# Loading the scan's row broadcasts through GpSimd's queue instead of SyncE's

## The chip, the cores and the metric

The kernel runs on one core of a Trainium2 chip. The metric is the device time of one execution in microseconds (us), as the median of several runs; lower is better. The engines are PE (TensorE, matmuls), DVE (VectorE), ACT (ScalarE), POOL (GpSimd) and SP (SyncE, which here issues DMAs only). Each engine works through its own queue in order; semaphores order the engines among themselves.

## The reference, cut to what matters

One layer of a bidirectional encoder on a sequence of 512 tokens with 1024 features, all in float32. The part that matters is branch A, a state-space scan in both directions with 32 heads in 4 groups, in chunks of 128 tokens:

```
a_cum  = cumsum(dt * a_head)                 # within a chunk, for each head and direction
decay  = exp(where(lower, a_cum[l] - a_cum[s], -inf))
y_diag = einsum(c.b, decay, x * dt)          # inside a chunk
y_off  = einsum(c, h_in, exp(a_cum))         # from the state that enters the chunk
y      = y_fwd + y_bwd + d_skip * x
```

Around it stand one wide input projection, a depthwise convolution, windowed attention, a gated merge, cross-attention into a memory of 256 tokens, and a feed-forward block.

## The kernel before, in words

**Weights.** Every weight block is 128 x 1024 float32 (512 KB). `load` (line 117) fetches it by `nc.sync.dma_start` into a buffer `raw` (two of them), casts it to a high part `whi` (ACT, line 130) and takes the rest as `wlo` (DVE or POOL, line 131); three buffers each. `mac` (line 135) multiplies with three matmuls per 128 x 128 block (lines 140 to 142). A load is written two weights ahead of the step that uses it.

**Projections of the scan.** `conv` (line 401) reads a projection from PSUM with one ACT instruction and four of DVE (`cvu`, line 409), then a tanh. PSUM has three banks for such projections, so PE waits when DVE has not emptied one.

**The rows.** `dt_step` writes the cumulated decays of all 64 (head, direction) pairs, 64 x 512, to DRAM as `adr`, and their exponentials as `edr`. In the scan these are read back, broadcast over partitions:
- `rows(h)` (line 510) loads for one head both directions of `adr` into `rt`, 128 x 2 x 512 (512 KB), with three buffers (`RB = 3`). `head` (line 526) asks for it, masks each direction on POOL (`affine_select`, line 532) and exponentiates on ACT (eight instructions, line 539). `both` (line 542) adds the directions on POOL into `mt` (line 545), which frees the `rt` buffer. `times` multiplies on DVE (line 550), and `inner` (line 554) feeds PE (line 560).
- `earows(i)` (line 517) loads `edr` for two heads into the two halves of `ear`, two DMAs of 64 x 2 x 512 (256 KB each), two buffers. `gather` (line 576) multiplies and adds them to the output `vv` on DVE and POOL (lines 584 and 585), which frees the buffer.

POOL also makes the weighted inputs `xw` of the state (line 490), sums of `bs` (line 643) and some squares, and it issues the twelve stores of the cross-attention's keys and values, `kdr` and `vdr` (lines 259 and 279).

**Order.** For each of the four groups, the scan's steps are woven by hand (`order`, `weave`) with the projections of the next group, the gates, and the output projection of the group before. The instructions are then laid into each engine's queue by a planner that simulates the kernel's times: of the instructions that are ready for an engine at that time, the earliest written goes first. So an instruction's place in a queue depends on the times that the planner expects. All loads before the change, weights and rows, stand in SP's one queue.

Of the kernel before, what the change touches and what calls it, by code (L numbers as in the profile page):

```python
# [15 lines left out]
P = 128  # L16
D = 1024
S = 512
# [55 lines left out]
def bidir_hybrid_layer(ctx: ExitStack, tc: tile.TileContext, io, dbg=None):  # L74
    nc = tc.nc
# [16 lines left out]
    adr = dram.tile([64, S], F32, tag="adr", name="adr")  # L92
    edr = dram.tile([64, S], F32, tag="edr", name="edr")
# [390 lines left out]
    def group_scan(g):  # L484
# [25 lines left out]
        def rows(h):  # L510
            rt = st["sp"].tile([P, 2, S], F32, tag="rt", name="rt", bufs=RB)
            e0 = 8 * g + h
            nc.sync.dma_start(rt, adr.rearrange("(d e) s -> e d s", d=2)[e0:e0 + 1].broadcast_to([P, 2, S]))
            st["rt", g, h] = rt


        def earows(i):
            def f():
                st["ear", i] = ear = st["sp"].tile([P, 2, S], F32, tag="ear", name="ear", bufs=2)
                for k in range(2):  # L520
                    e0 = 8 * g + 2 * i + k
                    nc.sync.dma_start(ear[64 * k:64 * k + 64], edr.rearrange("(d e) s -> e d s", d=2)[e0:e0 + 1]
                                      .broadcast_to([64, 2, S]))
            return f

        def head(h):
            def f():
                for n in (range(RB) if h == 0 else [h + RB - 1] if h + RB - 1 < HPG else []):
                    rows(n)
                rt = st["rt", g, h]  # L530
                for d in range(2):
                    nc.gpsimd.affine_select(  # L532
                        out=rt[:, d].rearrange("p (c l) -> p c l", c=NCH),
                        in_=rt[:, d].rearrange("p (c l) -> p c l", c=NCH), pattern=[[0, NCH], [1 - 2 * d, P]],
                        base=0, channel_multiplier=2 * d - 1, compare_op=ALU.is_ge, fill=neg)
                for d in range(2):
                    for c in range(NCH):
                        r, e0 = rt[:, d, c * P:(c + 1) * P], 32 * d + 8 * g + h
                        nc.scalar.activation(r, r, AF.Exp, bias=st["nb"][:, c, e0:e0 + 1])  # L539
            return f  # L540
# [690 lines left out]
```

## Time and profile before

| | |
|---|---|
| median of 3 runs | 1307.06 us (1306.88 to 1308.92) |
| the profiled execution | 1304.91 us |
| its span, first to last instruction | 1303.1 us |
| mean granted TensorE clock | 0.991 |
| busy: PE | 1251.0 us (96% of the span) |
| busy: DVE, ACT, POOL | 772.1 (59%), 564.3 (43%), 313.2 (24%) us |
| bytes moved by DMA | 143.48 MB, mean 110 GB/s |

The scan lies between about 90 and 510 us. Times in the rows are us from the start of the span, unless marked ns. A busy time counts computing instructions; issuing a DMA is not counted as busy. "<-" behind a wait names what ended it. The granted clock is given as a share of TensorE's full 2.4 GHz.

### The profile page before, as it was taken

The numbers are of one execution on the slowest core, as the hardware profiler recorded it, in microseconds if no ns is written. First come the engines' busy times: TensorE is split into PE (matmuls) and PEld (weight loads), VectorE is DVE, ScalarE is ACT, GpSimd is POOL, SyncE is SP. The second block draws the span as 40 slices with busy tenths as digits, with TensorE's granted clock in tenths as the row PEclk, the third lists the DMA queues.
The fourth block names the chain that finished last, engine by engine and source line by source line (L and its number), as shares of the span: only waits on it lengthen the run. The fifth ranks groups of instructions, "written<-read, shape, count | busy, mean of one in ns | idle before, by whom it ended". The sixth has DMA issues, their size and how long they took to land.

```text
span 1303.1 us, 16244 instructions
## 1 busy us (share of the span) xinstructions
PE 1251.0 (96%) x6076; PEld 1011.3 (78%) x6076; DVE 772.1 (59%) x1226; ACT 564.3 (43%) x1062; POOL 313.2 (24%) x259
## 2 busy tenths in 40 slices
PE   6988999999999999999999999999999999999996
PEld 5776678778778688877667888888888888888886
DVE  5874797677778865688874345675444444432323
ACT  6546655365465232358883234444332222222220
POOL 2344552442671732210000002001111111110001
PEclk9998999999999999999999999999999999999998
DMA  6447364445354232330104333422223222333331
GB/s 228 160 119 196 130 188 148 120 153 141 106 153 137 81 114 80 120 97 33 50 27 139 99 103 107 126 65 65 97 92 98 94 98 95 98 98 94 94 97 65
DMA packets 49614, 143.48 MB, mean 110 GB/s; under 512 B 5120, under 2 KB 8576, under 8 KB 49536
## 3 DMA queue, kind: packets, MB, share of 16 engines
q1 hardware_dynamic: 47248, 138.32, 34.7%
q10 hardware_dynamic: 1584, 2.03, 0.5%
q0 software_dynamic: 704, 2.10, 0.4%
q8 instruction: 48, 0.79, 0.3%
q14 instruction: 30, 0.25, 0.1%
HBM read 137.97 MB, written 4.46 MB: 109 GB/s over the span
## 4 chain that ended last, share of the span: by engine, by line
PE 59%; issue 6%; DVE 2%; ACT 1%; POOL 1%; DMA 0%; DVEq 0%; POOLq 0%; ACTq 0%
PE mm L140 18%; PE mm L142 18%; PE mm L141 18%; PE sb L818 1%; PE sb L805 1%; POOL rsw L717 1%; PE sb L992 1%; PE sa L961 1%; PE sa L777 1%; PE sa L779 0%; PE sb L172 0%; PE sb L572 0%; ACT whi L130 0%; PE sb L155 0%; ACT rsw L716 0%
## 5 line engine op out<-in xcount | busy, mean ns | idle before, releaser
L130 ACT CAST whi<-raw 128x1024 fp32r<-128x1024 f32 (+2 forms) x192 | 198.9, 1036 | 452.3 <-PE mm L141 359.4
L140 PE MATMUL mm<-hh,whi 128*128 128x512 f32 x968 | 382.9, 396 | 11.8 <-DVE cvu L409 11.1
L142 PE MATMUL mm<-hh,wlo 128*128 128x512 f32 x968 | 379.9, 393 | 0.0
L141 PE MATMUL mm<-hl,whi 128*128 128x512 f32 x968 | 379.8, 392 | 0.0
L131 DVE TENSOR_TENSOR wlo<-raw,whi 128x1024 fp32r<-128x1024 f32 (+2 forms) x193 | 238.2, 1235 | 145.0 <-ACT whi L130 135.2
L140 PEld LDWEIGHTS mm<-hh,whi 128*128 128x128 f32 x968 | 182.5, 189 | 52.0 <-issue 8.0
L142 PEld LDWEIGHTS mm<-hh,wlo 128*128 128x128 f32 x968 | 182.4, 188 | 38.9 <-issue 1.8
L141 PEld LDWEIGHTS mm<-hl,whi 128*128 128x128 f32 x968 | 182.7, 189 | 37.1 <-issue 1.1
L539 ACT ACTIVATE rt<-rt,nb 128x128 f32<-128x128 f32 x256 | 78.8, 389 | 67.4 <-POOL rt L532 67.3
L187 POOL TENSOR_TENSOR sq_acc<-sq_acc,sq 128x512 f32<-128x512 f32 x14 | 24.4, 1744 | 259.0 <-ACT sq L186 259.0
L1045 POOL TENSOR_TENSOR fa<-fa,row 128x512 f32<-128x512 f32 x22 | 39.1, 1779 | 192.3 <-ACT fa L1044 192.3
L140 PE MATMUL mm<-vh,whi 128*128 128x512 f32 (+1 forms) x192 | 71.1, 370 | 6.8 <-DVE cvu L409 2.7
L409 DVE SCALAR_TENSOR_TENSOR cvu<-mm,hcw,cvu 128x510 f32<-128x510 f32 (+1 forms) x96 | 71.4, 743 | 5.3 <-ACT cvu L406 3.8
L140 PE MATMUL mm<-fh,whi 128*128 128x512 f32 (+1 forms) x198 | 72.4, 366 | 0.0
L141 PE MATMUL mm<-fl,whi 128*128 128x512 f32 (+1 forms) x198 | 72.4, 365 | 0.0
L142 PE MATMUL mm<-fh,wlo 128*128 128x512 f32 (+1 forms) x198 | 72.4, 365 | 0.0
L142 PE MATMUL mm<-vh,wlo 128*128 128x512 f32 (+1 forms) x192 | 70.7, 368 | 0.0
L141 PE MATMUL mm<-vl,whi 128*128 128x512 f32 (+1 forms) x192 | 68.8, 358 | 0.0
L532 POOL TENSOR_SCALAR_AFFINE_SELECT rt<-rt 128x512 f32<-128x512 f32 x64 | 47.6, 766 | 67.7 <-DMA rt<-adr 67.5
L1047 DVE TENSOR_TENSOR ft<-fa,mm 128x512 f32<-128x512 f32 x22 | 15.1, 688 | 72.5 <-PE mm L142 70.4
L141 PE MATMUL mm<-ol,whi 128*128 128x512 f32 x128 | 50.0, 391 | 0.0
L142 PE MATMUL mm<-oh,wlo 128*128 128x512 f32 x128 | 50.0, 391 | 0.0
(231 smaller groups left out, 1953.7 us busy)
## 6 DMA issues: line engine op xcount, KB each, us to landing
raw<-in_w_in SPq DMA_DIRECT2D x69, 512.0 KB, 3.5
raw<-in_w_fi SPq DMA_DIRECT2D x44, 512.0 KB, 3.5
rt<-adr SPq DMA_DIRECT2D x32, 512.0 KB, 5.5
ear<-edr SPq DMA_DIRECT2D x32, 256.0 KB, 4.5
raw<-in_w_bs SPq DMA_DIRECT2D x16, 512.0 KB, 3.4
raw<-in_w_fo SPq DMA_DIRECT2D x16, 512.0 KB, 3.5
raw<-in_w_xk SPq DMA_DIRECT2D x8, 512.0 KB, 3.9
raw<-in_w_ba SPq DMA_DIRECT2D x8, 512.0 KB, 3.4
```

The lines of the kernel that those rows point to most:

```text
L130: nc.scalar.copy(hi[:, t], raw[:, t])
L131: (nc.gpsimd if i in LO_POOL else nc.vector).tensor_tensor(lo[:, t], raw[:, t], hi[:, t].bitcast(F32), op=ALU.subtract)
L140: nc.tensor.matmul(acc, wh, xh[:, k0 + k], start=first and k == 0, stop=False)
L141: nc.tensor.matmul(acc, wh, xl[:, k0 + k], start=False, stop=False)
L142: nc.tensor.matmul(acc, wl, xh[:, k0 + k], start=False, stop=last and k == nk - 1)
L187: eng.tensor_tensor(acc, acc, sq, op=ALU.add)
L409: nc.vector.scalar_tensor_tensor(u[:, b], acc[:, a], w5[j], u[:, b], op0=ALU.mult, op1=ALU.add)
L532: nc.gpsimd.affine_select(out=rt[:, d].rearrange("p (c l) -> p c l", c=NCH), in_=rt[:, d].rearrange("p (c l) -> p c l", c=NCH), pattern=[[ ...
L539: nc.scalar.activation(r, r, AF.Exp, bias=st["nb"][:, c, e0:e0 + 1])
L717: nc.gpsimd.tensor_tensor(sw, sw, st["ca"][:, S:2 * S], op=ALU.mult)
L1045: nc.gpsimd.tensor_tensor(a, a, st["row2"], op=ALU.mult)
L1047: nc.vector.tensor_tensor(t, a, st["fp", 2 * j + 1], op=ALU.mult)
```

## The change: two lines name another engine

The DMAs of `rows` and `earows` are issued by GpSimd's queue (POOL). Sources, destinations, sizes, buffers and the rest of the kernel are the same. SP's queue keeps the weights (and, outside the scan, the inputs and other loads that it had).

```diff
@@ -510,7 +510,7 @@
         def rows(h):
             rt = st["sp"].tile([P, 2, S], F32, tag="rt", name="rt", bufs=RB)
             e0 = 8 * g + h
-            nc.sync.dma_start(rt, adr.rearrange("(d e) s -> e d s", d=2)[e0:e0 + 1].broadcast_to([P, 2, S]))
+            nc.gpsimd.dma_start(rt, adr.rearrange("(d e) s -> e d s", d=2)[e0:e0 + 1].broadcast_to([P, 2, S]))
             st["rt", g, h] = rt
@@ -519,7 +519,7 @@
                 st["ear", i] = ear = st["sp"].tile([P, 2, S], F32, tag="ear", name="ear", bufs=2)
                 for k in range(2):
                     e0 = 8 * g + 2 * i + k
-                    nc.sync.dma_start(ear[64 * k:64 * k + 64], edr.rearrange("(d e) s -> e d s", d=2)[e0:e0 + 1]
+                    nc.gpsimd.dma_start(ear[64 * k:64 * k + 64], edr.rearrange("(d e) s -> e d s", d=2)[e0:e0 + 1]
                                       .broadcast_to([64, 2, S]))
             return f
```

## Rows read from the trace of the kernel before

**Rows 1.** Busy time by stretch: start:end, length, each engine's busy us (instructions), clock, DMA, GB/s.
```profile
90.00:510.00 420.00, 399.57 (x2078) 319.63 (x2078) 306.72 (x396) 209.69 (x446) 183.67 (x168) 0.99 0.47 137
```
The engines are PE, PEld, DVE, ACT and POOL, in this order.

**Rows 2.** PE's waits from 85 to 515 us: who for whom, total us, times, longest.
```profile
PE mm L140 <- DVE cvu L409: 9.1, 2, 6.4
...
PE sb L498 <- POOL xw L490: 2.3, 2, 2.0
PE mm L140 <- DVE cvt L642: 2.3, 4, 1.4
...
PE sa L560 <- DVE mt L550: 1.0, 2, 0.8
```

**Rows 3.** Busy time by stretch, the stretches with idle time of PE.
```profile
113.00:126.00 13.00, 6.60 (x24) 5.22 (x23) 7.00 (x10) 10.02 (x29) 6.58 (x8) 0.74 0.54 146
...
136.00:150.00 14.00, 11.67 (x57) 7.11 (x56) 13.21 (x17) 7.13 (x15) 11.82 (x10) 1.00 0.40 134
...
345.00:362.00 17.00, 15.04 (x89) 11.86 (x88) 12.37 (x15) 10.96 (x29) 11.96 (x13) 1.00 0.64 166
362.00:378.00 16.00, 13.32 (x71) 10.85 (x71) 12.46 (x15) 9.68 (x28) 13.26 (x12) 0.89 0.43 115
```

**Rows 4.** DMA issues (ns min/median/max, first and last start), and us from issue to landing.
```profile
L513 SPq DMA_DIRECT2D rt<-adr x32: 359/377/594, 91.7 to 436.8; - x32
...
L522 SPq DMA_DIRECT2D ear<-edr x32: 574/586/1795, 93.2 to 459.2; - x32
...
L259 POOL DMA_DIRECT2D kdr<-xw x8: 542/562/588, 59.2 to 172.3; - x8
...
DMA to landing us min/median/max: 4.5/5.5/11.9
```
The last line is that of the tile rt.

**Rows 5.** Waits of SP's queue from 90 to 510 us.
```profile
SPq L122 <- DVE wlo L131: 215.1, 50, 11.0
SPq L522 <- POOL vv L585: 62.2, 13, 8.9
SPq L513 <- POOL mt L545: 57.3, 24, 7.2
```

**Rows 6.** POOL's costliest group from 85 to 515 us: busy, mean ns, idle before, releaser.
```profile
L532 POOL TENSOR_SCALAR_AFFINE_SELECT rt<-rt 128x512 f32<-128x512 f32 x64 | 47.6, 766 | 67.7 <-DMA rt<-adr 67.5
```

**Rows 7.** In order of time, 98 to 120 us: start, us, instruction, idle before it.
```profile
98.50 0.65 SPq L122 DMA_DIRECT2D raw<-in_w_in  x1
...
107.73 8.71 SPq L513 DMA_DIRECT2D rt<-adr  x3
...
110.76 1.05 ACT L130 CAST whi<-raw 128x1024 fp32r<-128x1024 f32 x1 [3.00 <-DMA raw<-in_w_in]
...
113.59 1.23 POOL L532 TENSOR_SCALAR_AFFINE_SELECT rt<-rt 128x512 f32<-128x512 f32 x2 [4.65 <-DMA rt<-adr]
114.79 1.26 POOL L545 TENSOR_TENSOR mt<-rt 128x512 f32<-128x512 f32 x1
...
116.08 1.10 DVE L550 TENSOR_TENSOR mt<-mt,cb 128x512 f32<-128x512 f32 x1 [2.36 <-POOL mt L545]
...
119.56 0.77 PE L140 MATMUL mm<-hh,whi 128*128 128x512 f32 x1 [6.40 <-DVE cvu L409]
```
A row with x3 covers the first start to the last end, waits between them included.

**Rows 8.** In order of time, 139 to 147 us.
```profile
139.08 0.38 SPq L513 DMA_DIRECT2D rt<-adr  x1
...
144.66 1.31 POOL L532 TENSOR_SCALAR_AFFINE_SELECT rt<-rt 128x512 f32<-128x512 f32 x2 [2.18 <-DMA rt<-adr]
145.94 1.04 POOL L490 TENSOR_TENSOR xw<-xk,wt 128x512 f32<-128x512 f32 x1
```

**Rows 9.** In order of time, 345 to 378 us: first and last row issue, and a wait.
```profile
351.32 0.36 SPq L513 DMA_DIRECT2D rt<-adr  x1
...
370.85 3.87 POOL L532 TENSOR_SCALAR_AFFINE_SELECT rt<-rt 128x512 f32<-128x512 f32 x4 [2.74 <-DMA rt<-adr]
...
377.69 0.37 SPq L513 DMA_DIRECT2D rt<-adr  x1
```

## The prediction

> **What bounds the kernel now.** I read the page first (TensorE, PE, is busy for 96% of the span), then a table by stage, then PE's waits in the stage that the change touches. The rows are loaded only in the scan, from 90 to 510 us: there PE is busy 399.57 of 420 us, so 20.4 us of idle time is all that any change of the scan could give back, beside what a lower clock costs [rows 1]. PE's waits there are not for weights: no wait on a weight cast stands in the list. They are for DVE (9.1 us for the convolution cvu, 2.3 for cvt, 1.0 for mt) and for POOL (2.3 for xw) [rows 2]. DVE is late where mt is late, and mt comes from POOL. So POOL's chain, landing of rt, mask (L532), exponential on ACT, sum mt (L545), sets most of PE's idle time, and POOL is the engine that gets the new work.
>
> The idle time lies in a few stretches [rows 3]: 113 to 126 us (PE 6.60 of 13, mean clock 0.74, so partly at 1.2 of 2.4 GHz), 136 to 150 (11.67 of 14) and 345 to 378 (15.04 of 17 and 13.32 of 16). In the last three POOL is already busy 11.82 of 14, 11.96 of 17 and 13.26 of 16 us.
>
> The first stretch shows both sides of the change [rows 7]. SP issues a weight at 98.50 only after three rt and four ear loads. ACT's cast of it runs at 110.76, after 3.00 us of waiting for the landing. That speaks for the change. But DVE's next convolution work stands behind an mt at 116.08 that waited 2.36 us for POOL; POOL had made that mt at 114.79, because it stood until 113.59 waiting (4.65 us) for an rt load issued at 107.73. PE starts again at 119.56, after 6.40 us. What ends last there is the row, not the weight.
>
> **The change part by part.** Moved: 32 rt and 32 ear issues. SP loses 32 x 0.377 + 32 x 0.586 = 30.8 us of issuing [rows 4] and the waits in front of them, 62.2 + 57.3 = 119.5 us [rows 5]. Weights stood behind those. But SP's longest wait is for a free raw buffer, 215.1 us in 50 waits on DVE's wlo [rows 5], and that stays; PE waits for no weight in the scan. I cost the weights' release at nothing on the path. Its cover is the weights being a buffer or more ahead; if that is gone, as at 110.76, what is late next is mt.
>
> Added: 64 issues in POOL's queue. Before shows POOL issuing loads of no kind, only stores, kdr at 0.542 to 0.588, median 0.562 us, of 128 rows [rows 4]. An rt load names 256 rows (128 partitions, two directions), an ear load 128. Bounds for rt: 0.54 (the smallest kdr issue) and 1.12 (twice 0.562 for twice the rows). I take 0.56 for both: on SP the rt issue, with twice the rows of an ear issue, is the cheaper one (0.377 against 0.586), so the price does not follow the rows. That is 64 x 0.56 = 35.8 us on POOL, which goes from 183.67 [rows 1] to about 219 of 420 us.
>
> Waits added on POOL: an rt buffer is freed by mt (L545) and an ear buffer by vv (L585), both on POOL itself, so the issue follows its own engine's work and waits for hardly anything new. Behind each issue stand mask, mt, xw, vv and bs sums; ACT waits for the masks, DVE for mt and vv, PE for xw.
>
> The landing of rt: 4.5 / 5.5 / 11.9 us by SP [rows 4]. Free of weights in its own queue it may come down to the minimum, 1.0 less; how a load from POOL's queue lands is shown by no row. The other end is a load that takes as much longer than now as the load of the first stretch was above the minimum, 113.59 - 107.73 - 4.5 = 1.4. I take no change of the median, except in the first stretch, where the weights of 98.50 and after stood in the same queue: there -1.3, close to the floor.
>
> The DMA page of the Trainium skill (DMA: Bandwidth & Descriptors, Latency and other measured facts) gives about 1 us to the first byte for a DMA issued from GpSimd and about 0.6 for SP, and no run here shows it for a load. By it, an estimate, the six rounds below would each be 0.4 us longer, and the time 2.4 us above my figure.
>
> The sum on the path, each a place where PE now waits and POOL's delay passes through:
> - 113 to 126: the rt that ends last lands an issue later, +0.56, and -1.3 for the queue: -0.7.
> - 136 to 150: the rt issued at 139.08 ends POOL's wait at 144.66, and xw at 145.94, for which PE waits, stands behind it [rows 8]: +0.56.
> - 345 to 378: nine issues, five of rt and four of ear, first and last in [rows 9]. POOL's 25.2 us become 30.3 of 33, while it also waits for landings, as 2.74 us at 370.85 [rows 9]. Three rounds of rt follow each other: 3 x 0.56 = 1.7; of the two ear pairs one is counted as standing ahead of an mt: 1.1. Together +2.8.
> - about 438: two issues ahead of the mt behind PE's 1.0 us [rows 2]: 2 x 0.56 = +1.1.
>
> The rest of the scan, where PE is busy throughout, takes the issues into POOL's own waits for rows (67.5 us [rows 6]) at no cost. Sum: -0.7 + 0.6 + 2.8 + 1.1 = +3.8 us. On the profiled execution, 1304.91 us (span 1303.1 and 1.8 around it), that is 1308.7; the median of the runs is 2.15 us above that execution, so 1307.06 + 3.8 = 1310.9. With 0.54 an issue and no ear pair counted it is about +2, with 1.12 an issue about +9: 1309 to 1316 for this case alone.
>
> **The rivals.** *Nothing moves.* POOL waited 67.5 us for rows [rows 6] and 35.8 us of issues fit in it. Weights were never late for PE. Against it: a wait that ends with a landing moves when the issue moves. Time: 1307.1. One rule leads to the same number: the Trainium skill (DMA: Bandwidth & Descriptors, Rules for kernel authors) says that spreading DMAs over SP, ACT and GpSimd only saves sequencer issue time. By that rule nothing is won but SP's 30.8 us, and that engine is not the bound; the rule leaves out that an in-order queue holds one load behind another's wait, which the trace does show, 119.5 us of it [rows 5].
>
> *Faster: the weights released close the first stall.* The weight of 98.50 is issued when its buffer is free, lands before ACT needs it, and ACT's 3.00 us and the order behind it fall away, the row landing sooner too. If all of the stretch at 113 goes: 6.40 us of idle time and, for 6.60 us of work at a clock of 0.74, 6.60 x 0.26 = 1.7: -8.1, so 1299.0. For it: the only long stall of PE has a late weight in it. Against: the chain ends with mt.
>
> *Much slower: POOL becomes the bound.* If an rt issue costs 1.12, POOL in 345 to 378 has 25.2 + 5 x 1.12 + 4 x 0.56 = 33.0 of 33 us; the 7.8 us it now stands idle there (33 - 25.2) turn into delay of mt, and PE, which waits in order, takes them: +7.8. Two issues at each of the other three places, 3 x 2 x 1.12 = 6.7. Together +14.5: 1321.6. It decides from an issue of about 1 us on.
>
> **How the numbers follow.** Chances: my case 0.42, nothing moves 0.22, faster 0.28, POOL the bound 0.08. Against no change only 0.2% or 2.6 us can be told: below 1304.4 is faster, above 1309.7 slower. My case is slower for 0.33 and the same for 0.09 of its 0.42; "nothing moves" gives 0.17 same, 0.03 slower and 0.02 faster; the faster rival 0.27 and 0.01 same; the last 0.08 slower. So faster 0.29, same 0.27, slower 0.44. The range goes from the faster rival's time to the end of the slow one, 1299 to 1321; the cases of both signs are likely, so my case's own is 1309 to 1316.
>
> **What would show it.** Right: POOL's DMA issues at about 0.56 us, 64 of them; no rt or ear in SP's queue; POOL's wait for rows about as long as before; PE's waits for xw, cvu and mt, 12.4 us now, a few us longer. The weights' rival is right if the 6.40 us stall is gone. The forecast is wrong, too, if the planner, which lays each engine's queue by the times that it expects, draws another order of PE's or DVE's work once the loads stand on POOL: then the stalls lie elsewhere.

## The result, and the profile after

The changed kernel takes 1316.42 us (median of 4 runs, 1315.89 to 1316.91), the kernel before beside it 1307.37 (1306.88 to 1308.92): +9.05 us, a ratio of 1.0066, 95% interval [1.0054, 1.0078]. The profiled execution took 1316.78 us, its span is 1314.9 (before: 1304.91 and 1303.1).

Busy time of the scan, for [rows 1] (PE, PEld, DVE, ACT, POOL), of the changed kernel:

```profile
90.00:510.00 420.00, 394.35 (x2052) 316.71 (x2051) 314.27 (x391) 210.16 (x446) 222.29 (x230) 0.99 0.47 135
```

PE lost 5.2 us of busy time there, POOL gained 38.6: the profile counts POOL's DMA issues as busy time, unlike SP's, so most of this gain is the issues themselves. PE's waits, for [rows 2] (who for whom: total, times, longest):

```profile
PE sa L560 <- DVE mt L550: 7.2, 4, 4.4
PE mm L140 <- DVE cvu L409: 5.9, 4, 2.3
PE mm L140 <- DVE cvt L642: 4.0, 5, 1.0
PE sb L498 <- POOL xw L490: 2.5, 1, 2.5
```

The single long wait for cvu (6.4 us before) is gone; waits for mt grew from 1.0 to 7.2 us. By stretch, for [rows 3], with one more stretch, 231 to 257 us, in which PE was busy for all of its 26 us before (first the new stretch before the change, then all five after it):

```profile
231.00:257.00 26.00, 26.00 (x141) 20.14 (x140) 20.33 (x28) 9.69 (x23) 11.47 (x11) 1.00 0.44 116
```
```profile
113.00:126.00 13.00, 10.28 (x58) 8.51 (x56) 7.76 (x11) 11.70 (x34) 8.77 (x10) 1.00 0.66 163
136.00:150.00 14.00, 13.19 (x73) 9.12 (x72) 14.00 (x19) 5.25 (x8) 9.05 (x9) 1.00 0.36 99
231.00:257.00 26.00, 20.53 (x106) 15.39 (x106) 20.09 (x25) 10.31 (x27) 17.23 (x19) 0.87 0.44 122
345.00:362.00 17.00, 14.21 (x80) 10.28 (x78) 14.50 (x17) 2.85 (x5) 12.00 (x11) 0.90 0.34 93
362.00:378.00 16.00, 15.52 (x99) 12.99 (x98) 12.11 (x15) 12.15 (x31) 13.44 (x14) 1.00 0.63 170
```

Three of the four stretches of [rows 3] got better. The new hole is at 231. The start of the n-th matmul of one trace against the n-th of the other (the same amount of PE's work, though not always the same instruction) says when the time went; the places are named by the time before. The changed kernel is 2.1 us late at 95 us. That is hardly the change's doing: the traces of all other kernels below are 0.8 to 2.5 us late there, as the profiled execution of before lay 2.5 us under its median. Then it is 2.1 us early at 178, 1.5 early at 230, 6.7 late at 251, 8.1 late at 525, and its last matmul is 9.8 late. The remaining 1.9 us of the span's 11.7 lie after the last matmul.

The issues and landings for [rows 4] (ns min/median/max, first and last start; then us from issue to landing, for rt and for ear):

```profile
L513 POOL DMA_DIRECT2D rt<-adr x32: 717/727/787, 93.0 to 413.4; - x32
...
DMA to landing us min/median/max: 4.9/5.9/9.7
```
```profile
L522 POOL DMA_DIRECT2D ear<-edr x32: 587/606/662, 95.2 to 476.4; - x32
...
DMA to landing us min/median/max: 3.9/5.1/12.6
```

An issue costs POOL 0.73 and 0.61 us, and an rt row lands 0.4 us later than from SP's queue before. The Trainium skill (DMA: Bandwidth & Descriptors, Latency and other measured facts) has a first byte 0.4 us later for a GpSimd DMA than for one of SP. No run here shows that by itself. The landing is counted from the start of the issue, which is 0.35 us longer on POOL, and the median does not stay with the queue: in the kernels below it lies between 5.2 and 6.1 us for rt from POOL and between 5.1 and 5.5 from SP.

SP's queue, for [rows 5], no longer waits for mt or vv; its wait for a free raw buffer took the place of those waits:

```profile
SPq L122 <- DVE wlo L131: 365.9, 56, 22.0
```

POOL's groups, for [rows 6] (busy, mean ns, idle before and what ended it):

```profile
L532 POOL TENSOR_SCALAR_AFFINE_SELECT rt<-rt 128x512 f32<-128x512 f32 x64 | 48.7, 782 | 45.7 <-DMA rt<-adr 40.6 <-PE sb L572 2.8 <-PE mm L142 2.1
...
L513 POOL DMA_DIRECT2D rt<-adr x32 | 23.5, 734 | 6.3 <-DMA adr<-x 5.1 <-POOL mt L545 1.2
L522 POOL DMA_DIRECT2D ear<-edr x32 | 19.4, 610 | 2.1 <-POOL vv L585 2.1
```

The first stall, for [rows 7]:

```profile
101.15 0.34 SPq L122 DMA_DIRECT2D raw<-in_w_in  x1
...
110.31 1.05 ACT L130 CAST whi<-raw 128x1024 fp32r<-128x1024 f32 x1 [7.67 <-DMA raw<-in_w_in]
```
```profile
116.46 0.47 PE L140 MATMUL mm<-hh,whi 128*128 128x512 f32 x1 [2.25 <-DVE cvu L409]
```

PE now waits 2.25 us in place of 6.40. But the weight, free of rows in its queue, went out at 101.15, not earlier than the 98.50 of before, and still took 9.2 us from issue to cast, beside three rt and four ear loads; ACT waited 7.67 us for it in place of 3.00. So the shorter stall is not the weight's doing. An experiment below shows what it was.

And the new hole, in order of time (start, us, instruction, idle before it):

```profile
231.70 2.97 POOL L545 TENSOR_TENSOR mt<-rt 128x512 f32<-128x512 f32 x2
...
234.64 2.02 POOL L490 TENSOR_TENSOR xw<-xk,wt 128x512 f32<-128x512 f32 x1
...
236.61 1.51 POOL L513 DMA_DIRECT2D rt<-adr  x2
...
244.34 2.52 POOL L532 TENSOR_SCALAR_AFFINE_SELECT rt<-rt 128x512 f32<-128x512 f32 x4 [6.22 <-DMA rt<-adr]
...
246.83 2.48 POOL L545 TENSOR_TENSOR mt<-rt 128x512 f32<-128x512 f32 x2
...
248.13 1.74 DVE L550 TENSOR_TENSOR mt<-mt,cb 128x512 f32<-128x512 f32 x1 [3.57 <-POOL mt L545]
...
249.92 1.97 PE L560 MATMUL sa<-mt,xk 128*64 128x128 f32 x14 [4.38 <-DVE mt L550]
```

Two rt buffers come free with the two sums at 231.70. SP would issue their loads at once; POOL first does the second sum and an xw, and issues both loads together from 236.61. They land at about 244, POOL waits 6.22 us for them, DVE 3.57 for POOL, PE 4.38 for DVE.

That is general. From the end of the sum that frees an rt buffer to the start of the load that takes it (29 pairs of each trace), the load went out 0.18 us late on average before (5.3 us in all) and 2.36 after (68.3 in all, 21 of 29 over 1 us).

And the planner drew another order. The longest list of instructions that both kernels keep in the same order, up to the end of the scan's block, holds 1950 of 2156 on PE, 385 of 503 on DVE, 400 of 522 on ACT; behind it the orders are the same.

### The profile page after: what moved, and what is told of

The parts are those of the page before. It is cut to its first block, busy times and chain, and to the rows that moved or that the text cites. A ratio compares the mean times of both kernels' runs of the same rounds, so it can differ in the third digit from the quotient of the medians.

```text
span 1314.9 us, 16197 instructions
## 1 busy us (share of the span) xinstructions
PE 1254.5 (95%) x6076; PEld 1015.6 (77%) x6076; DVE 781.4 (59%) x1226; ACT 564.2 (43%) x1062; POOL 353.0 (27%) x323
## 4 chain that ended last, share of the span: by engine, by line
PE 73%; DVE 9%; issue 7%; DMA 4%; ACT 4%; POOL 3%; DVEq 0%; SPq 0%; POOLq 0%; ACTq 0%
PE mm L140 22%; PE mm L141 21%; PE mm L142 21%; DVE wlo L131 2%; DVE cvu L409 2%; DMA rt<-adr 2%; DMA raw<-in_w_in 1%; PE sb L818 1%; ACT whi L130 1%; PE sb L498 1%; PE sb L805 1%; PE sb L992 1%; DVE mt L550 1%; PE sb L572 1%; PE sa L961 1%
## 5 line engine op out<-in xcount | busy, mean ns | idle before, releaser
L131 DVE TENSOR_TENSOR wlo<-raw,whi 128x1024 fp32r<-128x1024 f32 (+2 forms) x193 | 248.1, 1286 | 144.4 <-ACT whi L130 136.4
L539 ACT ACTIVATE rt<-rt,nb 128x128 f32<-128x128 f32 x256 | 78.7, 390 | 41.7 <-POOL rt L532 41.6
L545 POOL TENSOR_TENSOR mt<-rt 128x512 f32<-128x512 f32 x32 | 47.7, 1501 | 17.3 <-ACT rt L539 8.6
```

The source lines that it names most:

```text
L131: (nc.gpsimd if i in LO_POOL else nc.vector).tensor_tensor(lo[:, t], raw[:, t], hi[:, t].bitcast(F32), op=ALU.subtract)
L545: nc.gpsimd.tensor_tensor(mt, st["rt", g, h][:, 0], st["rt", g, h][:, 1], op=ALU.add)
```

## The experiments

To keep order and queue apart, a function lays each engine's queue (PE, DVE, ACT, POOL) in an order given by a list, in place of the planner; in the kernels with dummies SP's too. The order of before was not run from a list with nothing else changed; the nearest run, rt alone on POOL, took 1304.65 us from the planner and 1304.64 from a list (below). The function moves the numbers of the lines below it by 110 or 111 (L655 or L656 is then the sum L545), and kernels with dummies by some 135. "Old order" is the order of the kernel before, "new order" that of the changed kernel. Each theory stands with its expected time, as it was written before the run.

### The order of before, rows on POOL, and the order of after, rows on SP

```diff
+def pin(tc, nc):              # ORDER: the instructions of each engine, as before had them
+    for names in ORDER:
+        chain = [traced[n] for n in names]
+        for a, b in zip(chain, chain[1:]):
+            tc.add_manual_dep(b, a.name, info, reason="order")
...
         if i == cutat:
+            pin(tc, nc)
             blk.close()
...
-            nc.sync.dma_start(rt, adr...
+            nc.gpsimd.dma_start(rt, adr...
-                    nc.sync.dma_start(ear[64 * k:64 * k + 64], edr...
+                    nc.gpsimd.dma_start(ear[64 * k:64 * k + 64], edr...
```

> The rows are loaded from POOL's queue as in the changed kernel, but PE's, DVE's, ACT's and POOL's computing instructions of the scan are held, by order-only edges, in exactly the order of the kernel before. Theory Q (the queue itself: 64 issues in POOL's queue at 0.73 and 0.61 us, and landings 0.4 to 0.6 us later, delay mt and xw): slower than before by about as much as the change, 1312 to 1318. Theory O (the planner drew another order, and that order has the stalls): about 1307 or less, within 3 us of before; the first stall of 6.40 us should shrink, since the weight of 98.50 goes out earlier.

Measured 1342.85 us (1341.44 to 1344.81), ratio 1.0267 [1.0253, 1.0281], far above what either theory gave. The second kernel has the rows on SP, as before, and ORDER from the changed kernel:

```diff
+            pin(tc, nc)       # ORDER: as after had them; rows stay on nc.sync
             blk.close()
```

> The rows are loaded from SP's queue as before, but the computing instructions of the scan stand in exactly the order of the changed kernel. Theory Q: about 1307, since POOL issues nothing more. Theory O: 1313 to 1318, as the changed kernel, with PE's stall at an mt near 250 us again.

Measured 1311.16 us (1308.29 to 1313.37), ratio 1.0023 [1.0015, 1.0032]; before beside both took 1307.7. This lies between the two theories. So the move costs 35.1 us in the order in which the prediction summed it, and 5.3 in the planner's new order, which costs 3.4 by itself.

The two runs also settle what shrank the first stall of [rows 7]. First the new order with the rows on SP, then the old order with the rows on POOL:

```profile
99.34 0.71 SPq L232 DMA_DIRECT2D raw<-in_w_in  x1
...
116.40 0.47 PE L250 MATMUL mm<-hh,whi 128*128 128x512 f32 x1 [2.81 <-DVE cvu L519]
```
```profile
119.82 0.77 PE L250 MATMUL mm<-hh,whi 128*128 128x512 f32 x1 [5.23 <-DVE cvu L519]
```

With the weights still behind seven row loads the stall is 2.81 us and PE starts at 116.40, as in the changed kernel (116.46). With the weights free in the old order it stays at 5.23 us. It was the planner's new order that shortened it.

One place of the old order, where a load goes out late: first before (POOL and SP's row loads), then the kernel with the rows on POOL:

```profile
174.37 1.46 POOL L545 TENSOR_TENSOR mt<-rt 128x512 f32<-128x512 f32 x1 [1.52 <-PE sa L560]
...
175.85 0.38 SPq L513 DMA_DIRECT2D rt<-adr  x1
...
177.74 1.35 POOL L187 TENSOR_TENSOR sq_acc<-sq_acc,sq 128x512 f32<-128x512 f32 x1 [1.91 <-ACT sq L186]
...
179.04 2.26 POOL L545 TENSOR_TENSOR mt<-rt 128x512 f32<-128x512 f32 x1
```
```profile
184.96 1.28 POOL L655 TENSOR_TENSOR mt<-rt 128x512 f32<-128x512 f32 x1 [1.84 <-PE sa L670]
186.20 1.74 POOL L297 TENSOR_TENSOR sq_acc<-sq_acc,sq 128x512 f32<-128x512 f32 x1
187.90 2.27 POOL L655 TENSOR_TENSOR mt<-rt 128x512 f32<-128x512 f32 x1
190.12 1.46 POOL L623 DMA_DIRECT2D rt<-adr  x2
195.60 1.22 POOL L642 TENSOR_SCALAR_AFFINE_SELECT rt<-rt 128x512 f32<-128x512 f32 x2 [4.02 <-DMA rt<-adr]
```

SP issued the load 0.02 us after the sum that frees its buffer. On POOL it stands behind a square and another sum, from 186.24 to 190.12: 3.9 us late.

### The same two with the loads directly behind the instruction that frees their buffer

In POOL's list each rt load is moved directly behind the mt sum that frees its buffer, each pair of ear loads behind its vv:

```diff
 mt<-rt         (L545)
+rt<-adr        (L513)
 sq_acc, xw, the next mt, ...
-rt<-adr        (L513)
```

> As the run with the rows in POOL's queue and the order of the kernel before (1342.85), but each row load now stands in POOL's queue directly behind the instruction that frees its buffer (mt for rt, vv for ear), where the planner had put it 1.64 us later on average. Theory P (a load in a computing engine's queue goes out late, behind other work, and that is the price): most of the 35 us goes, 1308 to 1318. Theory I (the issue's own 0.73 and 0.61 us and the landing 0.3 to 0.6 us later are the price): most of it stays, 1333 or more.

> The changed kernel with its own order, but each row load directly behind the instruction that frees its buffer, where it stands 2.36 us later on average now. Theory P: from 1316.4 to 1307 to 1312. Theory I: 1314 to 1318, no change.

In the order of before 1325.44 us (1321.57 to 1327.56), ratio 1.0134 [1.0119, 1.0150], between the two theories; in that of after 1308.67 (1306.18 to 1313.60), ratio 1.0012 [1.0001, 1.0023], as theory P had it. Before beside both took 1307.55. Both send their rt loads 0.30 us after the sum (8.6 us over 29 loads). So lateness alone costs 17.4 us in the old order and 7.75 in the new one, with the same issues, queue and order of computing. The place at 231 us, on POOL, in the new order (the profiled execution is the slowest of its twelve, 1313.60 us):

```profile
230.48 1.28 POOL L656 TENSOR_TENSOR mt<-rt 128x512 f32<-128x512 f32 x1
232.05 0.79 POOL L624 DMA_DIRECT2D rt<-adr  x1 [0.30 <-POOL mt L656]
232.87 1.30 POOL L656 TENSOR_TENSOR mt<-rt 128x512 f32<-128x512 f32 x1
234.47 0.73 POOL L624 DMA_DIRECT2D rt<-adr  x1 [0.30 <-POOL mt L656]
235.22 1.06 POOL L601 TENSOR_TENSOR xw<-xk,wt 128x512 f32<-128x512 f32 x1
237.16 1.83 POOL L643 TENSOR_SCALAR_AFFINE_SELECT rt<-rt 128x512 f32<-128x512 f32 x2 [0.87 <-DMA rt<-adr]
```

POOL waits 0.87 us for a row where it waited 6.22, and the mask starts 6.68 us after the first sum in place of 12.64.

### Only rt on POOL, in the order of before, directly behind the sum

```diff
+            pin(tc, nc)       # order of before, rt behind its mt
...
-            nc.sync.dma_start(rt, adr...
+            nc.gpsimd.dma_start(rt, adr...
```

> Order of the kernel before; rt alone from POOL's queue, each directly behind its mt; ear stays with SP. Theory P: within 6 us of before, 1307 to 1313, the price of 32 issues of 0.73 us alone. Theory I: rt carries most of the 35 us of both, 1325 or more.

Measured 1321.45 us (1319.92 to 1322.82), ratio 1.0109 [1.0095, 1.0124]. Half of the issues cost 13.9 of the 17.9 us that both cost, more than theory P and less than theory I gave. What is left when nothing is late does not go by the number of issues.

### Dummies on POOL, rows on SP

What is left in the old order, 17.9 us: POOL's time, or the rows' way through its queue? The rows stay on SP, all five queues are as before, and behind each freeing instruction POOL issues a load of 256 (or twice 128) pieces of 80 bytes that nobody reads:

```diff
                 nc.gpsimd.tensor_tensor(mt, st["rt", g, h][:, 0], st["rt", g, h][:, 1], op=ALU.add)
+                dummy(adr, 8 * g + h, 1)      # nc.gpsimd.dma_start(scratch, adr row...)
...
                     eng.tensor_tensor(vv[:, t], vv[:, t], ear[:, d, t], op=ALU.add)
+                dummy(edr, 8 * g + 2 * i, 2)
```

> Order of all five queues as in the kernel before, real rows on SyncE's queue. Added on GpSimd's queue, directly behind each instruction that frees a buffer of rows: a dummy load of the same number of pieces (256, or two of 128) but of 80 bytes each, into a scratch tile that nobody reads. 64 dummy issues, estimated from the issues of the changed kernel at 0.6 to 0.73 us each, so about 40 us more on GpSimd. With the rows on GpSimd in this same order and directly behind the freeing instruction the time was 1325.4, with the rows on SyncE 1307.7. Theory A: what is left there (some 18 us) is the time that issuing takes from GpSimd, in an order that was drawn without it. Then this kernel comes out at 1320 to 1327. Rival B: what is left is the way of the rows themselves (they come later through that queue), and the dummies fall into waits that GpSimd has anyway: 1307 to 1311.

Measured 1325.04 us (1324.13 to 1327.14), ratio 1.0126 [1.0109, 1.0143] (before beside it 1308.9): what the real rows took on POOL's queue (1325.44). POOL's groups of dummies (busy us, mean ns):

```profile
L226 POOL DMA_DIRECT2D scr<-adr x32 | 23.5, 734 | 0.0
...
L226 POOL DMA_DIRECT2D scr<-edr x32 | 19.4, 608 | 0.0
```

42.9 us of issues, the same as the real ones, cost as much with the rows on SP. So the price is POOL's time, and I see none for the landing. The totals agree; the places do less so (by the n-th matmul the dummies are 11.1 us late at 358 us and 18.4 at 471, the rows 5.9 and 19.1).

With computing in place of issuing:

```diff
+                dummy(1)      # three nc.gpsimd.affine_select on a 128 x 80 scratch
...
+                dummy(2)      # six
```

> As the run with dummy loads, but behind each freeing instruction GpSimd does computing work in place of an issue: three small selections over a scratch tile behind a mask sum, six behind a gathering, estimated from the 128x512 selections (766 ns) at 0.15 to 0.25 us each, so 0.45 to 0.75 us for each row load in place of the 0.6 to 0.73 of an issue. Nothing is loaded. If GpSimd's time as such is the price, whatever fills it: 1318 to 1327. If it is the issuing that costs (its descriptors written, VectorE slowed beside it), the dummy loads are slow and this is 1307 to 1311. If neither costs, both are at 1307 to 1311.

Measured 1328.99 us (1327.40 to 1331.73), ratio 1.0156 [1.0139, 1.0174], above the range expected. The dummies were dearer than I had estimated:

```profile
L228 POOL TENSOR_SCALAR_AFFINE_SELECT scr<-scr 128x80 f32<-128x80 f32 x186 | 77.1, 415 | 9.6
```

So POOL's time has a price when it is spent on computing too. It is no straight line: 1.8 times the time for 1.2 times the loss (20.1 against 16.1 us), or 1.4 times, if the 1.9 us that the loads cost behind the scan (below) are left out.

The same dummy loads in the order of after, rows on SP:

```diff
+            pin(tc, nc, extra)   # order of after, dummies behind mt and vv
```

> Order of all queues as in the variant that has the changed kernel's order and the rows on SyncE (1311.16); added are the 64 dummy loads on GpSimd, directly behind the instructions that free a row buffer, as in the run with dummy loads in the order of before, where they cost 16.1 to 17.3 us, 1.9 of it at the very end: GpSimd's closing drain lasts 2.5 us with 12 loads or stores issued on it, 5.1 with 44 and 7.7 with 76, and the span ends 1.9 us later with 76. Theory M: the planner's new order has made room for GpSimd's issues, so here only the end and a little remain: 1312 to 1316. Rival N: GpSimd's time costs as much in any order that fills PE so far, and the rows win it back by standing apart from the weights: 1322 to 1328.

Measured 1333.65 us (1327.94 to 1334.09), ratio 1.0185 [1.0164, 1.0207]. My theory M, that the new order had made room for the issues, fell: they cost 22.5 us there as well, more than the rival gave them. Moving the rows themselves, with the same issues at the same places, ends at 1308.67, 25.0 us lower. What differs is SP's queue, where weights stand behind rows or not. ACT's waits for the landing of a weight point there in part:

```profile
ACT whi L266 <- DMA raw<-in_w_in: 24.9, 3, 12.3
```
```profile
ACT whi L241 <- DMA raw<-in_w_in: 8.3, 1, 8.3
```
```profile
ACT whi L240 <- DMA raw<-in_w_in: 12.1, 2, 6.6
```

(First the dummies with rows on SP, then the rows on POOL, then the rows on SP without dummies.) That the weights' freedom is worth the 25 us is not shown. By the n-th matmul the first two kernels stand 1.0 us apart at 110 us, 9.0 at 345 and 19.8 at 471; more than half of this grows behind 345 us, where ACT waits for a late weight only once in the first kernel (3.5 us), and not at all in the second. In the order of before the same exchange was worth nothing (1325.44 against 1325.04). What makes up the 25 us, and why the order decides it, stays open.

### Parts of the change, each in the order that the planner draws for it

Only rt, only ear, and only rt with its loads directly behind the sum:

```diff
-            nc.sync.dma_start(rt, adr...
+            nc.gpsimd.dma_start(rt, adr...
```

> Only the rt loads move to POOL, ear stays with SP; the planner draws its own order. Theory Q: 32 issues of 0.73 us = 23.3 of the 42.7 us of issuing, and all of the rt chain: 1312 to 1315. Theory O: no rule from the issues; any time between 1302 and 1318.

```diff
-                    nc.sync.dma_start(ear[64 * k:64 * k + 64], edr...
+                    nc.gpsimd.dma_start(ear[64 * k:64 * k + 64], edr...
```

> Only the ear loads move to POOL, rt stays with SP; own order. Theory Q: 32 issues of 0.61 us = 19.4 us, not on the rt chain: 1307 to 1310. Theory O: no rule from the issues; any time between 1302 and 1318.

```diff
+            pin(tc, nc)       # the order of the kernel with rt alone, rt behind its mt
```

> The decays' rows (rt) alone on GpSimd's queue, in that variant's own order of computing (it took 1304.65), with each rt load moved directly behind the sum that frees its buffer. There its loads went out 47.9 us late in total (29 loads), where the prompt kernels have 8.6. Theory P (late issue is the price of the move): 1299 to 1303. Rival: what that variant's order gains and loses lies in its stalls on other engines, late rows were covered: 1304 to 1306.

rt alone: 1304.65 us (1302.08 to 1307.30), ratio 0.9979 [0.9970, 0.9988]. ear alone: 1317.44 (1316.89 to 1318.65), 1.0073 [1.0060, 1.0085]. Both lie outside theory Q's ranges. They do not add up to the whole change, since each has an order of its own. rt alone and prompt: 1304.64 (1300.91 to 1307.12), 0.9970 [0.9957, 0.9982]. Its loads are 8.6 us late in all in place of 47.9, and nothing came of it, as the rival had it: late rows were covered there. These two are the only ones that beat the kernel before, by 0.2 to 0.3%.

All rows on ACT's queue:

```diff
-            nc.sync.dma_start(rt, adr...
+            nc.scalar.dma_start(rt, adr...
-                    nc.sync.dma_start(ear[64 * k:64 * k + 64], edr...
+                    nc.scalar.dma_start(ear[64 * k:64 * k + 64], edr...
```

> All rows from ACT's queue, weights alone with SP, POOL without any issue, order by the planner. If weights alone with SP are worth something by themselves, 1300 to 1305. Theory P: ACT is a computing engine too, and its in-order queue holds the issue behind casts and exponentials: the mean delay from freed buffer to issue is 1 us or more, and the time 1308 to 1325.

Measured 1307.01 us (1305.08 to 1311.07), ratio 0.9996 [0.9987, 1.0004]; rt loads went out 0.09 us late. Neither range held: ACT sent the rows at once, and weights alone with SP won nothing. The rule that I had weighed, the Trainium skill's (DMA: Bandwidth & Descriptors, Rules for kernel authors) that spreading DMAs over queues only saves issue time, fits this run on ACT, whose order is again its own. For POOL it leaves out POOL's time (16.1 us by the dummies in the old order) and the lateness (17.4 and 7.75 us).

## Why the prediction was right or wrong

The sign was right and the time lies in the range of 1299 to 1321, 0.4 us above my own case's 1309 to 1316. But +3.8 was a sum over the old order, and there the move costs 35.1. The planner's new order took back 26.4 of it. That the size is near is luck: two errors of opposite sign.

| median, us | old order | new order |
|---|---|---|
| rows on SP | 1307.37 (before) | 1311.16 |
| rows on POOL, late | 1342.85 | 1316.42 (the changed kernel) |
| rows on POOL, sent at once | 1325.44 | 1308.67 |
| rows on SP, dummy loads on POOL | 1325.04 (before beside it 1308.9) | 1333.65 |

- **The issue's price** was mis-sized: 0.73 and 0.61 in place of 0.56. With these the four places give -0.6 + 0.7 + (3 x 0.727 + 2 x 0.606 =) 3.4 + (2 x 0.727 =) 1.5 = +5.0. That is the small error. The places themselves did not carry the price: with the old order and the rows on POOL, PE gains 0.2 us up to the end of the first (95 to 126) and falls back by 3.3, 6.9 and 0.2 us in the others (136 to 150, 345 to 378, 436 to 450), 10.2 of the 34.5 us that it loses behind 95 us. The other 24 lie where the sum had nothing.
- **"The issue follows its own engine's work and waits for hardly anything new"** failed. It does not wait on a semaphore; it stands behind other work of POOL. A load went out 2.36 us late, which cost 7.75 us of time after; in the old order it was 1.64 us a load and 17.4 us of time. I had looked for what POOL's issue delays and not for what delays the issue.
- **"The rest of the scan takes the issues into POOL's own waits for rows at no cost"** failed. The dummy loads cost 16 to 17 us in the old order (1.9 of them after the scan, below), and 22.5 in the new one. POOL's waits of 67.5 us [rows 6] paid for a part only: with the rows on POOL and sent at once, in the old order, POOL's waits for rows are still 41.6 us. My reading, argued and not shown, is that buffer free, load, mask, exponential and sum follow each other, and what POOL does on that way comes later, wait included.
- **The weights' release at nothing** held in the order that was summed (1325.44 with the rows on POOL, 1325.04 with dummies in their place). In the new order it is open, within the 25.0 us above. The first stall did shrink, from 6.40 to 2.25 us, which was to be the faster rival's sign, but by the new order: with the rows on SP it is 2.81. So the sign could not tell the rival from the planner.
- **The landing** rose by 0.4 us in the median, inside my bounds; the runs show no price for it.
- **POOL the bound** was to decide from an issue of about 1 us on. The price stayed at 0.73, and POOL's time counted all the same.
- **The planner** was named as what would make the forecast wrong, and it did draw another order. It was given no case and no price, though it was the largest single term.

Of the 9.05 us, with 1307.7 as before: +3.4 the new order with rows on SP; -2.5 the rows on POOL's queue, sent at once (with +1.9 for the closing, below, already in it), which is not clear of noise, since the intervals of the two ratios overlap; +7.75 the lateness. That is 8.7. The order's share comes late: with the rows on SP the new order's kernel is 1.5 us late at 95 us, 1.6 at 378 and 5.7 at 471. What costs it there is open. The lateness shows most at 231: from 230 to 251 us the changed kernel falls back by 8.2 us, with its loads sent at once by 4.9.

## What to carry to other kernels

A load in a computing engine's queue is sent when that queue comes to it, not when its buffer is free (here 2.36 us late on POOL, 0.09 on ACT): put it directly behind the instruction that frees the buffer, and look at the gap between the two in the trace. It need not help: here it gave 17.4 and 7.75 us in two orders, and nothing with rt alone. Do not count an engine's idle time as free for work put into it: 42.9 us of issues on POOL, which waited 67.5 us for rows, cost 16.1 us. Where a planner lays the queues, compare a change in the old order and in the new one, for the order may be worth more than the change.

## What the runs showed of the hardware

POOL's closing drain, beside the last instructions of the program, takes longer with each DMA issued from POOL. In the trace's raw records (it is no row of a view) it lasts 2.5 us in the four kernels with 12 such DMAs, 5.1 in the four with 44 and 7.7 in the six with 76: 0.082 us each. With 76 it ends after SP's last waits, so from the last matmul to the end of the span it is 9.4 us or more in place of 7.5 with 12 or 44.

VectorE's subtraction L131 (128 x 1024 float32) is slower beside work of POOL. In the traces of all 14 kernels, from 85 to 520 us, it takes at most 1.23 us where POOL works beside it for no more than 0.1 us. Beside POOL's work single ones take up to 2.3 us in the five kernels with no L131 over 2.4 us: the four in which POOL issues nothing but its twelve stores, and the old order with late rows. In the other nine, all with loads issued by POOL, one to four of them take 2.4 to 4.1 us. In the means this is little: in the old order 1287 ns before, 1403 with dummy loads, 1325 with dummy computing, 1301 and 1328 with the rows on POOL, late and at once. They do not follow the loss in time (the late rows lose most), so this is not the price of POOL's time in the old order; in the new order it was not separated.
